# The opening of a one-layer flow-model step: transposing x one token tile at a time, with products of zeros ahead of and behind the first tile

## The chip, the cores and the metric

The kernel runs on one core of a Trainium2 chip, as one program with one launch. The metric is the device time of that core in microseconds (us), the median of several runs. TensorE (PE in the profile, with its weight loads as PEld) multiplies and transposes, VectorE (DVE), ScalarE (ACT) and GpSimd (POOL) do the elementwise work, and SyncE (SP) issues nearly all of the transfers between HBM and the on-chip memory.

## The reference

One trunk layer is applied to 128 context tokens and to 256 latent tokens, 384 in all, with a model width of 2048. Both groups have the same weights; each has its own modulation, computed from a condition vector. All of it is in 32-bit floats.

```python
mod = (silu(cond) @ ada_w + ada_b).reshape(6, 2048)      # one row set per group: cond = c_ctx, c
shift_a, scale_a, gate_a, shift_f, scale_f, gate_f = mod
h = rmsnorm(x, norm_w[0]) * (1 + scale_a) + shift_a
proj = h @ w_in                                          # q, k, v, o, gates, u
hm, C, n, m = mlstm_bidir(q, k, v, gates, C0, n0, m0)    # 8 heads x 128, both directions
hm = rmsnorm(hm, mlstm_norm_w) * sigmoid(o)
hp = pool_mixer(u, pool_w, pool_scale)                   # windows 2, 4, 8, 16
x = x + gate_a * rmsnorm(concat(hm, hp) @ w_out, norm_w[1])
h = rmsnorm(x, norm_w[2]) * (1 + scale_f) + shift_f
x = x + gate_f * rmsnorm(square(relu(h @ w1)) @ w2, norm_w[3])
```

The change touches only what stands ahead of the first products of `h @ w_in`: the transposes of x, the first parts of `silu(cond) @ ada_w`, and the order in which they come.

## The kernel before

Activations are kept transposed: 2048 channels are 16 tiles of 128 channels on the partitions, with the 384 tokens along the free axis. x arrives as three token tiles of 128 tokens by 2048 channels (`xtok`, 1 MB each: the context tokens, then two tiles of latent tokens). `transpose_x(k)` makes channel tile k: three TensorE transposes, one from each token tile, into one PSUM bank `xt`, and then one copy of 128x384 into `xT`, on VectorE for even k and on ScalarE for odd k. So every channel tile needs all three token tiles.

Each product of 32-bit floats with a weight is three products: the weight is split into a high and a low part (`hi` by ScalarE, line 135, `lo` by VectorE, line 136), and so is the activation (`hh`, `hl`).

The first stretch of the program computes `u` and `v`, two column ranges of `h @ w_in`, in eight steps s of two channel tiles each. A step has five chunks: `u` twice (512 columns), then `v` three times (3, 3 and 2 heads), 18 TensorE products each. Before a step's `h` there must be the modulation of its two channel tiles, which the generator `first_ada` computes: for channel tiles 0 and 1 eight loads of 512 KB of `ada_w` (four for the scale, then four for the shift), and for each load four products with the condition vectors on TensorE (line 257). After each four of these comes a copy `ada_sb` on ScalarE (line 269), two small products that turn the row into a column (line 273), and the additions into `mod` on VectorE (lines 281 and 286). For channel tiles 2 and 3 the same is done again with eight loads (`ada_raw_2`). The first four and the second four of these go through the same four buffers, so that each of the second four loads waits until TensorE has read the load before it out of its buffer.

`make_h` then multiplies `xT` with the scale and with 1/rms of each token (`hm`), adds the shift while splitting (`hh` on ScalarE, line 448, `hl` on VectorE, line 449), and the first `u` products follow (line 503). The 1/rms comes from the squares of x on ScalarE (line 389), is spread over the partitions by one product with a matrix of ones (`bc_rx`, line 209) and lies in `rbc`.

Until the first `u` products, the order on TensorE, VectorE and ScalarE is the order in which the code stands: the string `X_ORDER` interleaves `t` (transpose the next channel tile), `a` (the next step of `first_ada`) and `b` (`bc_rx` and its copy). Ten channel tiles are transposed there, two more inside `make_h`, and the last four after the first `u` chunk (`XT_AT = 0`). After that only TensorE's order is fixed by the code. `ADA_STEPS` says how many steps of `first_ada` follow each of the five chunks of step 0: four after the first chunk and four after the third. SyncE's queue, where all loads of x, `ada_w` and `w_in` stand one behind another, is ordered by the scheduler.

Of the kernel before, what the change touches and what calls it, by code (L numbers as in the profile page):

```python
# [30 lines left out]
XT_AT = 0  # L31
ADA_STEPS = (4, 0, 4, 0, 0)
X_ORDER = "tatatatattaatabata"
# [11 lines left out]
def hymba_kernel(  # L45
# [34 lines left out]
    nc.sync.dma_start(cc[:, 0, :], c_ctx.rearrange("(p j) -> p j", j=16))  # L80
    nc.sync.dma_start(cc[:, 1, :], c[0].rearrange("(p j) -> p j", j=16))
    nc.sync.dma_start(cst[:, 0:3], cs_src[:, 0:3])
# [4 lines left out]
    for t, src in zip(x_tok, (x_prompt[0], x_sample[0, 0:128], x_sample[0, 128:256])):  # L87
        nc.sync.dma_start(t, src)
# [16 lines left out]

    cT = adap.tile([P, 16, 38], F32, name="cT")
# [270 lines left out]
    ada0 = first_ada()  # L377
    pp = bank("pp")
    nc.tensor.transpose(pp[:, 0:96], prm[0:96, 1, :], ident[0:96, 0:96])
# [3 lines left out]

    ssq = const.tile([P, 3, 2], F32, name="ssq")
    junk = wp.tile([P, 1024], F32, tag="hi", name="junk", bufs=N_W)
    rx = const.tile([P, 3], F32, name="rx")
    for i in (0, 1, 2):
        for q in range(2):
            nc.scalar.activation(junk, x_tok[i][:, q * 1024:(q + 1) * 1024], AF.Square, accum_out=ssq[:, i, q:q + 1])

    xT_dram = dram.tile([P, KT, NTOK], F32, name="xT_dram")
    xT = []
    rbc = pre.tile([P, NTOK], F32, name="rbc")
    ss = const.tile([P, 3], F32, name="ss")
    nc.vector.tensor_reduce(ss, ssq, axis=AX.X, op=ALU.add)
    rstd_cols(rx, ss, 3, 1.0 / D)

    xt_late = []

    def transpose_x(k, later=False):  # L400
        ps = bank(f"xt_{k}")
        for i in range(3):
            nc.tensor.transpose(ps[:, i * P:(i + 1) * P], x_tok[i][:, k * P:(k + 1) * P], ident)
        t = slot(f"xT{k}")
        xT.append(t)

        def copy():
            if k % 2:
                nc.scalar.activation(t[:, 0:NTOK], ps[:, 0:NTOK], AF.Copy)
            else:  # L410
                nc.vector.tensor_copy(t[:, 0:NTOK], ps[:, 0:NTOK])

        if later:
            xt_late.append(copy)
        else:
            copy()
# [60 lines left out]
    def shift_rows():  # L477
        for _ in range(2):
            transpose_x(len(xT), True)
# [6 lines left out]
    for copy in xt_late:  # L486
        copy()
# [909 lines left out]
```

## Time and profile before

| | us |
|---|---|
| median of 3 runs (lowest, highest) | 1684.31 (1683.07, 1687.94) |
| the profiled execution's own time | 1684.17 |
| its span, first to last instruction | 1682.5 |
| TensorE busy in the span | 1654.3 (98%) |
| VectorE busy | 1340.3 (80%) |
| ScalarE busy | 751.3 (45%) |
| read from HBM | 308.61 MB |

The profile is of one execution. Each row of its time line gives the start and the length in us, the engine, the line of the kernel, the operation, the tiles written and read, and how many instructions were merged into the row; brackets hold the idle time of the engine ahead of it and what ended it. One product of plain 32-bit floats appears as two instructions of TensorE where it is not a transpose, so that the four products of one `ada` step are "x8". An instruction's length reaches to the end of its pipeline: in a run of equal ones, the distance between starts is what each costs.

### The profile page before, as it was taken

The numbers are of one execution on the slowest core, as the hardware profiler recorded it, in microseconds if no ns is written. First come the engines' busy times: TensorE is split into PE (matmuls) and PEld (weight loads), VectorE is DVE, ScalarE is ACT, GpSimd is POOL, SyncE is SP. The second block draws the span as 40 slices with busy tenths as digits, with TensorE's granted clock in tenths as the row PEclk, the third lists the DMA queues.
The fourth block names the chain that finished last, engine by engine and source line by source line (L and its number), as shares of the span: only waits on it lengthen the run. The fifth ranks groups of instructions, "written<-read, shape, count | busy, mean of one in ns | idle before, by whom it ended". The sixth has DMA issues, their size and how long they took to land.

```text
span 1682.5 us, 27870 instructions
## 1 busy us (share of the span) xinstructions
PE 1654.3 (98%) x10965; PEld 1581.4 (94%) x10965; DVE 1340.3 (80%) x2009; ACT 751.3 (45%) x1225; POOL 133.3 (8%) x185
## 2 busy tenths in 40 slices
PE   6999999999999999999999999999999999999997
PEld 3888999999999989989999999999999999999996
DVE  3677769898999959997897688988588588588688
ACT  5322355555443345543444444444444444445443
POOL 1000002221000024520000000000000000000120
PEclk9999999999999999999999999999999999999999
DMA  9999757786789954754546246444344443443653
GB/s 318 332 310 298 253 172 248 240 258 221 238 273 311 311 194 142 209 151 128 178 154 195 84 135 187 152 144 150 101 151 129 123 138 118 145 124 113 186 182 136
DMA packets 258099, 320.95 MB, mean 191 GB/s; under 512 B 14784, under 2 KB 223120, under 8 KB 257584
## 3 DMA queue, kind: packets, MB, share of 16 engines
q1 hardware_dynamic: 250688, 303.62, 57.1%
q0 software_dynamic: 5984, 13.78, 2.9%
q8 instruction: 86, 1.41, 0.4%
q10 hardware_dynamic: 1296, 1.77, 0.3%
q14 instruction: 45, 0.37, 0.1%
HBM read 308.61 MB, written 10.51 MB: 190 GB/s over the span
## 4 chain that ended last, share of the span: by engine, by line
PE 94%; DVE 3%; issue 1%; DMA 1%; ACT 0%; SPq 0%; POOL 0%; DVEq 0%; ACTq 0%; POOLq 0%
PE acc_w L145 10%; PE acc_w L144 10%; PE acc_w L146 10%; PE v L503 4%; PE y L1231 4%; PE y L1232 4%; PE y L1230 4%; PE u L503 4%; PE acc_wo L144 3%; PE acc_wo L145 3%; PE acc_wo L146 2%; PE y_yz L1231 2%; PE y_yz L1230 2%; PE y_yz L1232 2%; PE y L1074 2%; PE y L1073 2%
## 5 line engine op out<-in xcount | busy, mean ns | idle before, releaser
L145 PE MATMUL acc_w<-h2l,hi_w 128*128 128x384 f32 (+1 forms) x1024 | 346.2, 338 | 0.5 <-DVE h2l L1024 0.5
L144 PE MATMUL acc_w<-h2h,hi_w 128*128 128x384 f32 (+1 forms) x1024 | 344.2, 338 | 1.2 <-ACT h2h L1020 1.2
L146 PE MATMUL acc_w<-h2h,lo_w 128*128 128x384 f32 (+1 forms) x1024 | 345.1, 337 | 0.0
L136 DVE TENSOR_TENSOR lo_w<-raw_w,hi_w 128x1024 fp32r<-128x1024 f32 x152 | 185.3, 1220 | 136.5 <-ACT hi_w L135 136.3
L135 ACT ACTIVATE hi_w<-raw_w 128x1024 fp32r<-128x1024 f32 x152 | 160.8, 1058 | 213.7 <-PE acc_w L145 83.4
L317 DVE SCALAR_TENSOR_TENSOR ada_acc<-ada_raw,sg,ada_acc 128x1024 f32<-128x1024 f32 (+1 forms) x240 | 252.0, 1081 | 2.1 <-DMA ada_raw<-in_ada_w_dram 2.1
L144 PEld LDWEIGHTS acc_w<-h2h,hi_w 128*128 128x128 f32 x1024 | 192.2, 188 | 2.9 <-ACT h2h L1020 2.0
L145 PEld LDWEIGHTS acc_w<-h2l,hi_w 128*128 128x128 f32 x1024 | 192.6, 188 | 1.2 <-DVE h2l L1024 0.8
L146 PEld LDWEIGHTS acc_w<-h2h,lo_w 128*128 128x128 f32 x1024 | 192.4, 188 | 0.3 <-DVE lo_w L136 0.2
L1216 ACT ACTIVATE hi_t<-w 128x1024 fp32r<-128x1024 f32 x104 | 109.5, 1059 | 118.7 <-PE y L1232 34.0
L1217 DVE TENSOR_TENSOR lo_t<-w,hi_t 128x1024 fp32r<-128x1024 f32 x104 | 126.3, 1220 | 15.1 <-ACT hi_t L1216 14.7
L1217 DVE TENSOR_TENSOR lo_b<-w,hi_b 128x1024 fp32r<-128x1024 f32 x78 | 95.3, 1221 | 40.0 <-ACT hi_b L1216 39.8
L1216 ACT ACTIVATE hi_b<-w 128x1024 fp32r<-128x1024 f32 x78 | 82.5, 1060 | 97.0 <-PE acc_w L145 64.6
L135 ACT ACTIVATE hi_wo<-raw_wo 128x1024 fp32r<-128x1024 f32 x32 | 34.0, 1064 | 81.3 <-DMA raw_wo<-in_w_out_dram 64.0
L950 ACT ACTIVATE z<-acc_w 128x384 f32<-128x384 f32 x54 | 26.3, 487 | 74.8 <-PE acc_w L146 74.8
L503 PE MATMUL v<-hi_v,hh 128*128 128x384 f32 (+1 forms) x144 | 47.8, 332 | 0.0
L503 PE MATMUL v<-lo_v,hh 128*128 128x384 f32 (+1 forms) x144 | 46.5, 323 | 0.0
L503 PE MATMUL v<-hi_v,hl 128*128 128x384 f32 (+1 forms) x144 | 46.5, 323 | 0.0
L136 DVE TENSOR_TENSOR lo_wo<-raw_wo,hi_wo 128x1024 fp32r<-128x1024 f32 x32 | 38.8, 1218 | 7.3 <-ACT hi_wo L135 6.3
L986 POOL DMA_DIRECT2D gf_dram<-gfT x1 | 0.5, 521 | 551.9 <-DVE gfT L985 551.9
L144 PE MATMUL acc_k<-hh,hi_k 128*128 128x384 f32 x128 | 44.2, 345 | 0.0
L144 PE MATMUL acc_o<-hh,hi_o 128*128 128x384 f32 x128 | 43.9, 343 | 0.0
(2268 smaller groups left out, 4566.9 us busy)
## 6 DMA issues: line engine op xcount, KB each, us to landing
raw_w<-in_w_dram SPq DMA_DIRECT2D x152, 512.0 KB, 4.3
ada_raw<-in_ada_w_dram SPq DMA_DIRECT2D x130, 512.0 KB, 5.0
w<-in_w_dram SPq DMA_DIRECT2D x104, 512.0 KB, 4.4
raw_wo<-in_w_out_dram SPq DMA_DIRECT2D x32, 512.0 KB, 5.6
u<-in_ada_w_dram SPq DMA_DIRECT2D x18, 512.0 KB, 6.0
raw_u<-in_w_in_dram SPq DMA_DIRECT2D x16, 512.0 KB, 7.0
raw_q<-in_w_in_dram SPq DMA_DIRECT2D x16, 512.0 KB, 4.7
raw_k<-in_w_in_dram SPq DMA_DIRECT2D x16, 512.0 KB, 4.7
```

The lines of the kernel that those rows point to most:

```text
L135: nc.scalar.activation(hi[:, 0:n], raw[:, 0:n], AF.Copy)
L136: low = lambda: nc.vector.tensor_tensor(lo[:, 0:n], raw[:, 0:n], hi[:, 0:n].bitcast(F32), op=ALU.subtract)
L144: nc.tensor.matmul(ps, lh, rh, start=start, stop=False)
L145: nc.tensor.matmul(ps, lh, rl, start=False, stop=False)
L146: mm3.ins = nc.tensor.matmul(ps, ll, rh, start=False, stop=stop).ins
L317: nc.vector.scalar_tensor_tensor(acc[:, g, :], raw[:, a, :], cj, acc[:, g, :], op0=ALU.mult, op1=ALU.add)
L503: nc.tensor.matmul(acc[i][:, 0:n], h[k0 + k][a][:, i * P:(i + 1) * P], (hi, lo)[b][:, k, :], start=k == 0 and a + b == 0, stop=k == nk - 1 ...
L1216: nc.scalar.activation(hi, raw, AF.Copy)
L1217: nc.vector.tensor_tensor(lo, raw, hi.bitcast(F32), op=ALU.subtract)
L1230: nc.tensor.matmul(acc, xh, wh, start=start and j == 0, stop=False)
L1231: nc.tensor.matmul(acc, xh, wl, start=False, stop=False)
L1232: nc.tensor.matmul(acc, xl, wh, start=False, stop=stop and j == 3)
```

## The change

x's context tile is loaded first, ahead of the condition vectors, and the constants (the identity among them) come over ScalarE's queue instead of SyncE's. `rbc` is set to zero at the start, and six products of 128x384 zeros (`run_up(6)`) go to TensorE before x is there. `transpose_x(i, k0, on_act)` now takes one token tile i and four channel tiles: four transposes into one bank, then four copies of 128x128, and it is called for all 16 channel tiles of token tile 0, then (after two more products of zeros and the transposes of the parameters) of token tile 1, and then of tile 2. The sixteen copies of tile 0 are twelve on VectorE and four on ScalarE, those of tile 1 are all on VectorE, those of tile 2 are half and half. Only then come the steps of `first_ada`, with `bc_rx` after the third load's products. No transposes are left between or behind them. `ADA_STEPS` becomes (0, 4, 4, 0, 0): the four steps that followed the first `u` chunk now follow the second, and the other four still follow the first `v` chunk. The second `u` chunk's weights are therefore loaded ahead by one chunk only.

```diff
--- before.py
+++ after.py
@@ -28,9 +28,8 @@
 N_W = 4
 N_ADA = 4
 N_E = 1
-XT_AT = 0
-ADA_STEPS = (4, 0, 4, 0, 0)
-X_ORDER = "tatatatattaatabata"
+ADA_STEPS = (0, 4, 4, 0, 0)
+X_ORDER = "aaabaaaaaa"
 N_X = 4
 RATE_GF = 0.4
 RATE_GS = 0.25
@@ -77,15 +76,16 @@
     pre = pre_scope.enter_context(tc.tile_pool(name="pre", bufs=1))
     prm = pre.tile([P, 2, P], F32, name="prm")
     masks = vp.tile([P, N_CST - 3, P], F32, name="masks")
-    nc.sync.dma_start(cc[:, 0, :], c_ctx.rearrange("(p j) -> p j", j=16))
-    nc.sync.dma_start(cc[:, 1, :], c[0].rearrange("(p j) -> p j", j=16))
-    nc.sync.dma_start(cst[:, 0:3], cs_src[:, 0:3])
+    nc.scalar.dma_start(cst[:, 0:3], cs_src[:, 0:3])
 
     vsb = [vp.tile([P, NH, 129], F32, name=f"v{i}") for i in range(3)]
     gsb = vp.tile([P, 3, 32], F32, name="gsb")
     x_tok = [pre.tile([P, D], F32, tag=f"x{i}", name=f"xtok{i}") for i in range(3)]
-    for t, src in zip(x_tok, (x_prompt[0], x_sample[0, 0:128], x_sample[0, 128:256])):
-        nc.sync.dma_start(t, src)
+    nc.sync.dma_start(x_tok[0], x_prompt[0])
+    nc.sync.dma_start(cc[:, 0, :], c_ctx.rearrange("(p j) -> p j", j=16))
+    nc.sync.dma_start(cc[:, 1, :], c[0].rearrange("(p j) -> p j", j=16))
+    for i in (1, 2):
+        nc.sync.dma_start(x_tok[i], x_sample[0, (i - 1) * P:i * P])
     nc.gpsimd.dma_start(prm[0:96, 1, :], ada_b[0].rearrange("(r p) -> r p", p=P))
     nc.gpsimd.dma_start(prm[0:64, 0, :], norm_w[0].rearrange("i (k p) -> (i k) p", p=P))
     nc.gpsimd.dma_start(prm[64:72, 0, :], mlstm_norm_w[0].rearrange("(k p) -> k p", p=P))
@@ -103,6 +103,8 @@
     order.enter_context(tc.manual_schedule(engines={mybir.EngineType.PE, mybir.EngineType.DVE, mybir.EngineType.Activation}))
 
 
+    rbc = pre.tile([P, NTOK], F32, name="rbc")
+    nc.vector.memset(rbc, 0.0)
     cT = adap.tile([P, 16, 38], F32, name="cT")
     nc.vector.memset(cT, 0.0)
     sg = const.tile([P, 2, 16], F32, name="sg")
@@ -375,50 +377,54 @@
         yield from ada_rows([(0, k0, 2), (1, k0, 2)], ps)
 
     ada0 = first_ada()
+    ssq = const.tile([P, 3, 2], F32, name="ssq")
+    junk = wp.tile([P, 1024], F32, tag="hi", name="junk", bufs=N_W)
+    rx = const.tile([P, 3], F32, name="rx")
+    ss = const.tile([P, 3], F32, name="ss")
+    xT_dram = dram.tile([P, KT, NTOK], F32, name="xT_dram")
+    xT = [slot(f"xT{k}") for k in range(KT)]
     pp = bank("pp")
+
+    def run_up(n):
+        for _ in range(n):
+            nc.tensor.matmul(pp[:, 0:NTOK], rbc[:, 0:P], rbc, start=True, stop=True)
+
+    def squares(i):
+        for q in range(2):
+            nc.scalar.activation(junk, x_tok[i][:, q * 1024:(q + 1) * 1024], AF.Square, accum_out=ssq[:, i, q:q + 1])
+
+    def transpose_x(i, k0, on_act):
+        ps = bank(f"xt_{i}_{k0}")
+        for a in range(4):
+            nc.tensor.transpose(ps[:, a * P:(a + 1) * P], x_tok[i][:, (k0 + a) * P:(k0 + a + 1) * P], ident)
+        for a in range(4):
+            dst, src = xT[k0 + a][:, i * P:(i + 1) * P], ps[:, a * P:(a + 1) * P]
+            if on_act:
+                nc.scalar.activation(dst, src, AF.Copy)
+            else:
+                nc.vector.tensor_copy(dst, src)
+
+    run_up(6)
+    squares(0)
+    for q in range(4):
+        transpose_x(0, 4 * q, q == 3)
+    run_up(2)
     nc.tensor.transpose(pp[:, 0:96], prm[0:96, 1, :], ident[0:96, 0:96])
     nc.tensor.transpose(pp[:, 96:176], prm[0:80, 0, :], ident[0:80, 0:80])
     nc.vector.tensor_copy(prmT[:, 80:176], pp[:, 0:96])
     nc.vector.tensor_copy(prmT[:, 0:80], pp[:, 96:176])
-
-    ssq = const.tile([P, 3, 2], F32, name="ssq")
-    junk = wp.tile([P, 1024], F32, tag="hi", name="junk", bufs=N_W)
-    rx = const.tile([P, 3], F32, name="rx")
-    for i in (0, 1, 2):
-        for q in range(2):
-            nc.scalar.activation(junk, x_tok[i][:, q * 1024:(q + 1) * 1024], AF.Square, accum_out=ssq[:, i, q:q + 1])
-
-    xT_dram = dram.tile([P, KT, NTOK], F32, name="xT_dram")
-    xT = []
-    rbc = pre.tile([P, NTOK], F32, name="rbc")
-    ss = const.tile([P, 3], F32, name="ss")
-    nc.vector.tensor_reduce(ss, ssq, axis=AX.X, op=ALU.add)
-    rstd_cols(rx, ss, 3, 1.0 / D)
-
-    xt_late = []
-
-    def transpose_x(k, later=False):
-        ps = bank(f"xt_{k}")
-        for i in range(3):
-            nc.tensor.transpose(ps[:, i * P:(i + 1) * P], x_tok[i][:, k * P:(k + 1) * P], ident)
-        t = slot(f"xT{k}")
-        xT.append(t)
-
-        def copy():
-            if k % 2:
-                nc.scalar.activation(t[:, 0:NTOK], ps[:, 0:NTOK], AF.Copy)
-            else:
-                nc.vector.tensor_copy(t[:, 0:NTOK], ps[:, 0:NTOK])
-
-        if later:
-            xt_late.append(copy)
-        else:
-            copy()
+    squares(1)
+    for q in range(4):
+        transpose_x(1, 4 * q, False)
+    squares(2)
+    for q in range(4):
+        if q == 2:
+            nc.vector.tensor_reduce(ss, ssq, axis=AX.X, op=ALU.add)
+            rstd_cols(rx, ss, 3, 1.0 / D)
+        transpose_x(2, 4 * q, q >= 2)
 
     for op in X_ORDER:
-        if op == "t":
-            transpose_x(len(xT))
-        elif op == "a":
+        if op == "a":
             next(ada0)
         else:
             nc.vector.tensor_copy(rbc, bcast_row(rx, "rx")[:, 0:NTOK])
@@ -474,24 +480,15 @@
                     with tc.issue_after(load_w.ins):
                         nc.sync.dma_start(masks, cs_src[:, 3:N_CST])
 
-    def shift_rows():
-        for _ in range(2):
-            transpose_x(len(xT), True)
-        next(ada0)
-        for _ in range(2):
-            transpose_x(len(xT), True)
-
-    h_ins = make_h(0, shift_rows)
+    h_ins = make_h(0, lambda: next(ada0))
     lo_later[0]()
-    for copy in xt_late:
-        copy()
     order.close()
     order2 = ExitStack()
     order2.enter_context(tc.manual_schedule(engines={mybir.EngineType.PE}))
     for s in range(NS):
         for ci, (kind, c0, w) in enumerate(chunks):
             k0, nk = ksteps[s]
-            load_ahead(5 * s + ci, 1 if s + ci == 0 else N_AHEAD)
+            load_ahead(5 * s + ci, 1 if s == 0 and ci < 2 else N_AHEAD)
             hi, lo, n = loaded.pop(5 * s + ci)
             acc = [bank(f"{kind}_{c0}_{s}_{i}") for i in range(3)]
 
@@ -506,9 +503,6 @@
                         next(ada0, None)
             if s == ci == 0:
                 load_ahead(1, 1)
-            if s == 0 and ci == XT_AT:
-                while len(xT) < KT:
-                    transpose_x(len(xT))
             for _ in range((ADA_STEPS if s == 0 else (1, 1, 1, 0, 0))[ci]):
                 next(ada0, None)
             if ci == 3 and s < NS - 1:
```

The start of TensorE's queue, where L379 and L380 transpose the parameters, L403 (L399 after the change) x, and L257 (L259) multiplies a load of `ada_w`. Before:

```order
L379 MATMUL pp<-cst,prm 128x96
L380 MATMUL pp<-cst,prm 128x80
L403 MATMUL xt_139<-cst,xtok_89 128x128
L403 MATMUL xt_139<-cst,xtok_90 128x128
L403 MATMUL xt_139<-cst,xtok_91 128x128
L257 MATMUL ada_0_145<-ada_raw_0_0_146,cT 32x256 x4
```

and with the change:

```order
L390 MATMUL pp<-rbc 128x384 x6
L399 MATMUL xt_0_151<-cst,xtok_87 128x128 x4
L399 MATMUL xt_4_160<-cst,xtok_87 128x128 x4
L399 MATMUL xt_8_169<-cst,xtok_87 128x128 x4
L399 MATMUL xt_12_178<-cst,xtok_87 128x128 x4
L390 MATMUL pp<-rbc 128x384 x2
L412 MATMUL pp<-cst,prm 128x96
L413 MATMUL pp<-cst,prm 128x80
L399 MATMUL xt_0_195<-cst,xtok_88 128x128 x4
```

Every transpose of x now stands ahead of the first product with `ada_w`, and the first sixteen need only the context tile (`xtok_87`).

TensorE's queue between the first `u` chunk and the `v` chunks, before (a row of dots stands for further rows of the same chunk):

```order
L503 MATMUL u_0_2_312<-lo_u_0_259,hh_267 128x512
L403 MATMUL xt_337<-cst,xtok_89 128x128
...
L403 MATMUL xt_355<-cst,xtok_91 128x128
L257 MATMUL ada_2_361<-ada_raw_2_0_362,cT 32x256 x4
L257 MATMUL ada_2_361<-ada_raw_2_4_368,cT 32x256 x4
L257 MATMUL ada_2_361<-ada_raw_2_8_374,cT 32x256 x4
L257 MATMUL ada_2_361<-ada_raw_2_12_380,cT 32x256 x4
L503 MATMUL u_0_0_401<-hi_u_0_333,hh_262 128x512
...
L503 MATMUL v_0_0_432<-hi_v_0_391,hh_262 128x384
...
L257 MATMUL ada_2_361<-ada_raw_2_0_453,cT 32x256 x4
```

and with the change:

```order
L500 MATMUL u_0_2_373<-lo_u_0_344,hh_352 128x512
L500 MATMUL u_0_0_401<-hi_u_0_394,hh_347 128x512
...
L259 MATMUL ada_2_422<-ada_raw_2_0_423,cT 32x256 x4
L259 MATMUL ada_2_422<-ada_raw_2_4_429,cT 32x256 x4
L259 MATMUL ada_2_422<-ada_raw_2_8_435,cT 32x256 x4
L259 MATMUL ada_2_422<-ada_raw_2_12_441,cT 32x256 x4
L500 MATMUL v_0_0_469<-hi_v_0_452,hh_347 128x384
...
L259 MATMUL ada_2_422<-ada_raw_2_0_490,cT 32x256 x4
```

The twelve transposes are gone from there, and only one chunk (`v`, 18 products) is left between the first four and the second four `ada_2` steps, where there were two.

SyncE's queue at the loads of these second four steps (`ada_raw_2`), before:

```order
L129 DMA raw_v_0_425<-in_w_in_dram 128x2x256
L129 DMA raw_v_0_425<-in_w_in_dram 128x2x32
L253 DMA ada_raw_2_0_453<-in_ada_w_dram 128x4x256
L253 DMA ada_raw_2_4_459<-in_ada_w_dram 128x4x256
L253 DMA ada_raw_2_8_465<-in_ada_w_dram 128x4x256
L253 DMA ada_raw_2_12_471<-in_ada_w_dram 128x4x256
L129 DMA raw_u_1_482<-in_w_in_dram 128x2x512
```

and with the change:

```order
L131 DMA raw_v_0_462<-in_w_in_dram 128x2x256
L131 DMA raw_v_0_462<-in_w_in_dram 128x2x32
L368 DMA u_335<-in_ada_w_dram 128x4x256
L255 DMA ada_raw_2_0_490<-in_ada_w_dram 128x4x256
L255 DMA ada_raw_2_4_496<-in_ada_w_dram 128x4x256
L255 DMA ada_raw_2_8_502<-in_ada_w_dram 128x4x256
L255 DMA ada_raw_2_12_508<-in_ada_w_dram 128x4x256
L131 DMA raw_u_1_519<-in_w_in_dram 128x2x512
```

One load of 512 KB of a later step (`u_335`, part of the modulation of channel tiles 4 and 5, which goes to a spare place) now stands ahead of the second four; it stood seven places further behind.

## The prediction

> **What bounds the kernel now.** First the page: how busy TensorE is, and what the chain of work that ended last consists of.
>
> ```profile
> span 1682.5 us, 27870 instructions
> PE 1654.3 (98%) x10965; PEld 1581.4 (94%) x10965; DVE 1340.3 (80%) x2009; ACT 751.3 (45%) x1225; POOL 133.3 (8%) x185
> PE   6999999999999999999999999999999999999997
> PE 94%; DVE 3%; issue 1%; DMA 1%; ACT 0%; SPq 0%; POOL 0%; DVEq 0%; ACTq 0%; POOLq 0%
> ```
>
> TensorE bounds everything but the first slice (42 us) and the last. So the opening can give back at most what TensorE waits there. Next the waits of TensorE in the whole run, longest first:
>
> ```profile
> PE xt L403 <- DMA xtok<-in_x_sample_dram: 4.8, 2, 2.8
> PE pp L379 <- DMA cst<-in_consts_dram: 4.5, 1, 4.5
> PE pp L380 <- DMA prm<-in_pool_scale_dram: 4.0, 1, 4.0
> ...
> PE ada L257 <- DMA ada_raw<-in_ada_w_dram: 1.1, 1, 1.1
> ```
>
> These four, 14.4 us together, are all transfers of the opening. Third, busy time of each engine by stage, with the granted clock, the DMA share and GB/s at the end of a row:
>
> ```profile
> 0.00:16.29 16.29, 1.92 (x5) 0.84 (x5) 2.23 (x10) 7.60 (x13) 4.70 (x15) 1.00 0.85 282
> 16.29:30.00 13.71, 13.09 (x108) 6.67 (x108) 5.56 (x16) 5.11 (x11) 0.89 (x1) 1.00 1.09 356
> 37.50:45.00 7.50, 7.50 (x40) 6.48 (x36) 2.50 (x3) 4.81 (x9) 0.00 (x0) 1.00 1.03 336
> ```
>
> TensorE does 1.92 us of work in the first 16.29 us and almost never rests afterwards. But the DMA engines are full from 16 us on, at some 350 GB/s. Two queues are therefore nearly level in the opening, and work taken from TensorE counts only where the transfers are ahead of it. Fourth, TensorE's time line:
>
> ```profile
> 14.73 0.47 PE L403 MATMUL xt<-cst,xtok 128*128 128x128 f32 x1 [1.98 <-DMA xtok<-in_x_sample_dram]
> 16.32 1.08 PE L257 MATMUL ada<-ada_raw,cT 128*32 128x256 f32 x8 [1.11 <-DMA ada_raw<-in_ada_w_dram]
> 19.18 0.90 PE L403 MATMUL xt<-cst,xtok 128*128 128x128 f32 x3
> 23.15 0.64 PE L257 MATMUL ada<-ada_raw,cT 128*32 128x256 f32 x8
> 23.72 0.55 PE L403 MATMUL xt<-cst,xtok 128*128 128x128 f32 x3
> 25.38 0.91 PE L209 MATMUL bc_rx<-dg_rx,cst 128*128 128x384 f32 x2 [0.55 <-DVE dg_rx L207]
> 27.27 0.64 PE L257 MATMUL ada<-ada_raw,cT 128*32 128x256 f32 x8
> 29.84 1.83 PE L503 MATMUL u<-hi_u,hh 128*128 128x512 f32 x6
> 34.29 1.47 PE L403 MATMUL xt<-cst,xtok 128*128 128x128 f32 x12
> 35.69 1.93 PE L257 MATMUL ada<-ada_raw,cT 128*32 128x256 f32 x32
> 37.55 0.50 PE L503 MATMUL u<-hi_u,hh 128*128 128x512 f32 x1
> 41.84 0.34 PE L503 MATMUL v<-hi_v,hh 128*128 128x384 f32 x1
> 45.10 1.94 PE L257 MATMUL ada<-ada_raw,cT 128*32 128x256 f32 x32
> 46.97 0.44 PE L503 MATMUL v<-hi_v,hh 128*128 128x384 f32 x1
> ```
>
> The same eight `ada` instructions take 1.08 us at 16.32 and 0.64 at 23.15, three transposes 0.90 and 0.55: until some 20.5 us TensorE runs at 0.6 of its later rate, though the clock column says 1.00. It had worked without a rest since 16.3.
>
> **The first term: when the first u product starts.** It needs the last `ada` load, the first `raw_u` and the split of both.
>
> ```profile
> 27.84 0.88 PE L403 MATMUL xt<-cst,xtok 128*128 128x128 f32 x6
> 28.32 1.05 ACT L135 ACTIVATE hi_u<-raw_u 128x1024 fp32r<-128x1024 f32 x1
> 29.39 1.50 ACT L448 ACTIVATE hh<-hm,mod 128x128 fp32r<-128x128 f32 x4
> ```
>
> For the transfer, the answer for `raw_u` from 19.3 to 20 us:
>
> ```profile
> L129 SPq DMA_DIRECT2D raw_u<-in_w_in_dram x1: 1412/1412/1412, 19.3 to 19.3; - x1
> DMA to landing us min/median/max: 8.8/8.8/8.8
> ```
>
> Issued at 19.31 it landed at 28.1, was split from 28.32 on, ScalarE went on to `hh` at 29.39, and u started at 29.84. So u starts 1.75 us behind that landing, and the transposes that are taken away between 17 and 29 us gain nothing there: they already stood in the shadow of the transfers. What can move u is the stream itself.
>
> ```profile
> 0.81 0.38 SPq L80 DMA_DIRECT2D cc<-in_c_ctx_dram  x1
> 2.18 0.43 SPq L88 DMA_DIRECT2D xtok<-in_x_prompt_dram  x1
> 36.39 2.02 SPq L253 DMA_DIRECT2D ada_raw<-in_ada_w_dram  x4
> ```
>
> x's context tile takes the place of the first small load, 0.81 instead of 2.18, so the whole stream behind it can come up to 1.37 us earlier. The constants still have to come (192 KB, 0.5 us at 356 GB/s), on another queue but through the same engines. Bounds are 0 (other transfers set the pace of the first 10 us) and 1.37; I take 1.2, nearer to the issue rows. u starts at 28.64.
>
> **What hides the added work.** x's tiles 0 and 1 were there when their squares began:
>
> ```profile
> 7.68 1.06 ACT L389 ACTIVATE junk<-xtok 128x1024 f32<-128x1024 f32 x1 [2.94 <-DMA xtok<-in_x_prompt_dram]
> 12.32 1.06 ACT L389 ACTIVATE junk<-xtok 128x1024 f32<-128x1024 f32 x1 [2.31 <-DMA xtok<-in_x_sample_dram]
> ```
>
> Six products of zeros: `bc_rx`, the same shape, took 0.91 us, at the slow rate 0.91 x 1.08/0.64 = 1.5. From 1.5 us on (behind a memset) they end between 7 and 10.5, about when x's tile 0 is there (7.7 before, 6.5 by the shift). 32 transposes of tiles 1 and 2 cost 32 x 0.55/3 = 5.9 us, eight `ada` steps 5.1, `bc_rx` and the small products some 2: 13 us from tile 1 at some 11 us (12.3 - 1.2), done by 24; the last `ada` load, one load of 1.4 us ahead of `raw_u`, comes at 28.1 - 1.4 - 1.2 = 25.5. Without that cover (all at the slow rate) it is 13 x 1.69 = 22 us, done at 33. The copies:
>
> ```profile
> L411 DVE COPY xT<-xt 128x384 f32<-128x384 f32 x8 | 4.4, 555 | 5.0 <-PE xt L403 4.9
> L409 ACT ACTIVATE xT<-xt 128x384 f32<-128x384 f32 x8 | 3.8, 485 | 10.9 <-PE xt L403 10.9
> L381 DVE COPY prmT<-pp 128x96 f32<-128x96 f32 x1 | 0.3, 256 | 3.4 <-PE pp L380 3.4
> ```
>
> Sixteen copies of 128x384 become 48 of 128x128; between the 256 ns of 96 columns and the 555 of 384, one of 128 is about 290. VectorE gets 36, 10.4 us at most, done by some 20 us; then `dg_rx` and `bc_rx` follow by 22, and 1/rms is not needed before `hm`, at about 25. Hidden by 3 us; it would cost only what exceeds them.
>
> **The second term: behind the first u chunk.** Twelve transposes vanish: 35.69 - 34.29 = 1.40 us. With 1.2 that is a lead of 2.6 us. The chunks' costs are distances of starts: u 34.29 - 29.84 = 4.45, second u 41.84 - 37.55 = 4.29, four `ada` steps 37.55 - 35.69 = 1.86, v 45.10 - 41.84 = 3.26. Now u runs from 28.64 to 33.09, the second u to 37.38 (its VectorE split no longer stands behind two copies), the first four `ada_2` steps to 39.24, v to 42.50.
>
> **The third term: where the lead goes.** The second four `ada_2` steps come next, at 42.50 instead of 45.10. But their loads wait until TensorE has emptied the four buffers, which before began at 35.69 and now begins at 37.38, 1.69 us later. The answer for these loads from 36.3 to 38 us:
>
> ```profile
> L253 SPq DMA_DIRECT2D ada_raw<-in_ada_w_dram x4: 368/457/458, 36.4 to 37.9; - x4
> DMA to landing us min/median/max: 4.0/5.8/7.6
> ```
>
> Before: the first issued at 36.39 landed at 40.4 (4.0), the last issued at 37.95 at 45.6 (7.6), and its products were the last quarter of the row at 45.10, starting at 46.5: 0.9 us to spare. With the change: the first lands at 42.1, the last at 45.6 + 1.69 = 47.3, and TensorE, ready for it at 42.50 + 1.4 = 43.9, waits some 3.4 us in all. The last step takes 0.46, and the next v chunk starts at 47.7 instead of 46.97: 0.8 later. Against that: these four queued behind other loads before, and need 1.5 us each at the stream's rate, which is 4.0 + 3 x 1.5 = 8.5 us from the first issue (36.39 + 1.69 = 38.08) to the last landing, 46.6, where 45.6 - 36.4 = 9.2 were seen. Then the chunk starts at 47.0, as before. One further load of 512 KB now stands ahead of them; it fills the time in which SP waits, so I give it nothing (1.5 us if it is late). Between 0 and +0.8 I take +0.4. Behind this point TensorE has no wait on the opening; everything moves by that amount.
>
> **Sum.** -1.2 (stream) - 1.4 (transposes) + 3.0 (wait for the second four; between 2.6 and 3.4) = +0.4 us on the profiled execution's 1684.17, which is its span of 1682.5 and 1.7 around it, and 0.14 below the median: 1684.6. This is no change: for this kernel, about 0.3% (5 us) is what a measurement can tell, and the three runs of before lie 4.9 us apart.
>
> **The rivals.** *The lead is kept.* If the second four land in time, by an earlier stream or a shorter way than 4.0 us, all 2.6 us stay: 1681.6. For it speaks that TensorE waits for nothing later in the opening; against it the buffer rule: the first issue can't come before the first of the four steps has read its load, 38.08, and the last load cannot then be there at 43.9. Chance 0.12.
>
> *TensorE is slow again when u starts.* Its work between tile 2 and u is thin, eight steps of 0.64 in some 12 us. If it falls back to the slow rate, u's first 4.5 us (the stretch from 16.3 to about 20.8 before the rate rose) do some 2.2 us less, the second four loads go out 2.2 later still, and the time is 1686.8. Against it: between 22 and 29 us work was also broken (0.55 idle ahead of `bc_rx`) and the rate held. Chance 0.12. The Trainium skill, "TensorE: Matmul & The Clock Gate", Part 4, says that transposes do not count as activity for the clock; Part 1 says that an idle window of about 3.4 us throttles it. By it the 32 transposes would undo what the zeros bring, which makes this rival likelier; no row here separates transposes from the `ada` products beside them.
>
> *The slow rate lasts until u; the other side.* If neither zeros nor transposes raise the rate, the work of 13 us behind tile 1 takes 22, and before it eight zeros (12.3 us) and 16 transposes (4.8) end at some 18.6 instead of 11: the last `ada` step ends at 41 instead of 27.9, and u starts some 13 us late: 1697, slower than before by more than a measurement's reach. It decides once TensorE is still slow at 18 us. Against it: 4.5 us of steady work sufficed before. Chance 0.03.
>
> **How the numbers follow.** 0.73 for the forecast. The forecast and the first two rivals (0.97) lie within 5 us of before, the third rival (0.03) above. Of the 0.97 I leave 0.03 below and 0.02 above to drift between measurements, as the three runs of before show it: faster 0.03, same 0.92, slower 0.05. The range, 1681.5 to 1687.3, holds the first two rivals and the spread of before's runs.
>
> **What would show it.** Right: first u product at 28.3 to 29.8; three transposes at 0.55 us or `ada` steps at 0.64 well ahead of 20 us; no transposes behind 20 us; a new wait of TensorE for `ada_raw` of 2.5 to 3.5 us between 42 and 47.5; the third chunk's successor (the second v) at 46.5 to 47.8. Wrong: no such wait and the second v at 44.5 (first rival); `ada` steps of 1.08 behind 20 us (second and third). Anything beyond 5 us would have to come from behind the opening, where TensorE's order is the same.

## The result, and the profile after

The change made the kernel slower: a median of 1692.13 us (1691.1 to 1696.05, 6 runs) against 1684.43 (1683.07 to 1687.94, 6 runs) before, a ratio of 1.0047 with an interval of 1.0036 to 1.0059, so 6 to 10 us. The forecast was 1684.6, its range ended at 1687.3. The profiled execution took 1691.1, its span is 1689.4, 6.9 above the span before.

TensorE's waits in the whole run, after (us in total, times, longest):

```profile
PE ada L259 <- DMA ada_raw<-in_ada_w_dram: 5.9, 7, 2.4
```

The long waits for x, the constants and the parameters, 13.3 us in the first three rows of before, are down to 1.4 for x; what TensorE waits for most is now `ada_raw`, 5.9 us in seven waits (1.1 in one before). Now the stages of the opening, cut where the granted clock changes (length, busy time of TensorE, of its weight loads, of VectorE, ScalarE and GpSimd, granted clock, DMA share, GB/s):

```profile
16.75:20.17 3.42, 2.14 (x26) 0.61 (x18) 1.74 (x8) 1.50 (x10) 0.88 (x1) 1.00 1.10 349
20.17:23.58 3.41, 2.21 (x26) 0.86 (x24) 1.65 (x6) 0.38 (x1) 0.00 (x0) 1.00 1.11 350
23.58:33.82 10.24, 8.20 (x37) 4.65 (x38) 4.61 (x9) 3.77 (x7) 0.00 (x0) 0.50 1.08 357
...
37.50:45.00 7.50, 7.50 (x61) 5.75 (x60) 2.58 (x3) 4.19 (x7) 0.00 (x0) 1.00 0.52 175
...
47.47:50.89 3.42, 1.07 (x16) 0.32 (x16) 0.00 (x0) 0.00 (x0) 0.00 (x0) 1.00 1.05 375
50.89:54.30 3.41, 3.41 (x15) 3.19 (x11) 0.00 (x0) 1.44 (x2) 0.00 (x0) 0.50 1.08 363
```

The clock falls to a half twice: for 10.24 us from 23.58 on, and for 3.41 from 50.89 on. (Up to its first rise, at 6.51 here, the column reads 1.00 although the rate is the slow one.) Ahead of each fall TensorE had little to do, 2.21 of 3.41 us and 1.07 of 3.42; but the stretch from 16.75 on, with 2.14, was followed by none, so the busy time alone does not decide (last section). And between 37.5 and 45 the transfers, full before (1.03, 336 GB/s), are half idle. TensorE's time line:

```profile
21.71 0.61 PE L275 MATMUL ada<-cst,ada_sb 128*128 128x2 f32 x4 [0.50 <-ACT ada_sb L271]
22.25 0.64 PE L259 MATMUL ada<-ada_raw,cT 128*32 128x256 f32 x8
23.56 1.08 PE L259 MATMUL ada<-ada_raw,cT 128*32 128x256 f32 x8 [0.67 <-DMA ada_raw<-in_ada_w_dram]
...
28.09 1.02 PE L275 MATMUL ada<-cst,ada_sb 128*128 128x2 f32 x4 [0.56 <-ACT ada_sb L271]
29.86 2.93 PE L500 MATMUL u<-hi_u,hh 128*128 128x512 f32 x6 [0.76 <-ACT hh L454]
...
35.96 0.40 PE L500 MATMUL u<-hi_u,hh 128*128 128x512 f32 x1
...
40.25 1.93 PE L259 MATMUL ada<-ada_raw,cT 128*32 128x256 f32 x32
42.11 0.44 PE L500 MATMUL v<-hi_v,hh 128*128 128x384 f32 x1
...
45.48 1.13 PE L259 MATMUL ada<-ada_raw,cT 128*32 128x256 f32 x16
48.97 0.64 PE L259 MATMUL ada<-ada_raw,cT 128*32 128x256 f32 x8 [2.36 <-DMA ada_raw<-in_ada_w_dram]
50.46 0.72 PE L259 MATMUL ada<-ada_raw,cT 128*32 128x256 f32 x8 [0.85 <-DMA ada_raw<-in_ada_w_dram]
51.11 0.69 PE L500 MATMUL v<-hi_v,hh 128*128 128x384 f32 x1
```

Read along the places that the prediction named. u starts at 29.86 (before 29.84). Its chunk takes 6.10 us (29.86 to 35.96; before 4.45), because its first 4 us run at half clock. The first `v` starts at 42.11 (41.84), the second four `ada_2` steps at 45.48 (45.10). There TensorE waits 2.36 and 0.85, the second `v` chunk starts at 51.11 (46.97) and runs at half clock until 54.30. The first product of step 1, the first `u` row behind 50 us, before and after:

```profile
53.05 0.39 PE L503 MATMUL u<-hi_u,hh 128*128 128x512 f32 x1
```

```profile
58.62 0.39 PE L500 MATMUL u<-hi_u,hh 128*128 128x512 f32 x1
```

So the opening loses 5.57 us. The parts are u's slow start +1.65, the transposes -1.40, the wait +3.21, the way from the second `v` chunk to step 1, partly at half clock, +1.4 (7.51 in place of 6.08), and small rests, +0.7. SyncE's queue shows why the transfers pause:

```profile
34.65 0.46 SPq L368 DMA_DIRECT2D u<-in_ada_w_dram  x1
40.95 2.02 SPq L255 DMA_DIRECT2D ada_raw<-in_ada_w_dram  x4
```

From 35.1 to 40.95 it issues nothing: the first of the second four loads waits for its buffer, until TensorE has begun the first four steps (40.25, 0.70 ahead of the issue; before 35.69 and 36.39, also 0.70), and all loads behind it wait with it.

### The profile page after: what moved, and what is told of

Same layout as the page of the kernel before. It is cut to its first block, busy times and chain, and to the rows that moved or that the text cites. A ratio compares the mean times of both kernels' runs of the same rounds, so it can differ in the third digit from the quotient of the medians.

```text
span 1689.4 us, 27939 instructions
## 1 busy us (share of the span) xinstructions
PE 1665.9 (99%) x10981; PEld 1589.4 (94%) x10981; DVE 1343.8 (80%) x2038; ACT 748.8 (44%) x1229; POOL 133.3 (8%) x185
## 4 chain that ended last, share of the span: by engine, by line
PE 85%; DVE 7%; issue 3%; DMA 3%; POOL 1%; SPq 1%; ACT 1%; DVEq 0%; POOLq 0%; ACTq 0%
PE acc_w L147 10%; PE acc_w L146 10%; PE acc_w L148 10%; PE v L500 4%; PE y L1225 4%; PE y L1226 4%; PE y L1224 4%; PE u L500 4%; PE acc_wo L146 3%; PE acc_wo L147 3%; PE acc_wo L148 3%; DVE ada_acc L319 2%; PE y_yz L1225 2%; PE y_yz L1224 2%; PE y_yz L1226 2%
```

## The experiments

The theory formed on this profile: two losses, added. **Thin work**: without the transposes, TensorE has only eight short steps between 17 and 29 us, the clock falls, and u starts slow. (Before, eight channel tiles were transposed among the steps of `X_ORDER` and four in `make_h`, not ten and two as the kernel's description above has it.) **Buffers**: with one chunk instead of two between the two sets of four steps, the second four loads come late; TensorE waits, and the clock falls again. The rivals: that one of them is the whole loss, or that the eight products of zeros do harm. The edits are shown in excerpts; a row of dots stands for what is left out.

**Old places of the `ada_2` steps.**

```diff
-ADA_STEPS = (0, 4, 4, 0, 0)
+ADA_STEPS = (4, 0, 4, 0, 0)
...
-            load_ahead(5 * s + ci, 1 if s == 0 and ci < 2 else N_AHEAD)
+            load_ahead(5 * s + ci, 1 if s + ci == 0 else N_AHEAD)
```

> The changed kernel with the four ada steps back behind the first u chunk (4, 0, 4, 0, 0) and the loads ahead as before; its opening of x and zeros stays. Theory A (two causes: the clock falls before u, and the second four ada loads come too late): u starts at 29.9 and its first chunk still takes 6.1 us because the clock is low from 23.6 to 33.8, but the wait of 3 to 4 us ahead of the second v chunk is gone, and with it the second fall of the clock at 51; that chunk starts at 47 to 48 instead of 51.1, and the time is 1685.5 to 1687.5. Rival (the clock in the opening is nearly all of the loss): within 1.5 us of the changed kernel, above 1690.

Measured: 1689.06 us (1685.05 to 1690.26, 10 runs) against 1685.03, ratio 1.0016 (1.0007 to 1.0026). Two stages of the opening, and from the time line the first product of step 1:

```profile
26.56:36.79 10.23, 8.26 (x27) 5.99 (x28) 3.96 (x7) 3.76 (x7) 0.00 (x0) 0.50 1.01 327
36.80:60.00 23.20, 23.20 (x166) 18.95 (x165) 11.00 (x23) 13.96 (x27) 0.00 (x0) 1.00 0.94 307
```

```profile
55.17 0.39 PE L500 MATMUL u<-hi_u,hh 128*128 128x512 f32 x1
```

The first fall stays, 3 us later than in the change (u's chunk, from 30.62 to 37.81, loses 2.7); the wait and the second fall are gone: TensorE is busy without a gap from 36.8 to 60. Step 1 starts 2.12 later than before, in place of 5.57.

**Zeros as cover**, the steps as changed: one product of zeros (`zz`, 128x384) behind each `ada` step, the last one ahead of the first `u` product.

```diff
-X_ORDER = "aaabaaaaaa"
+X_ORDER = "azazazbazazazazazaz"
...
+        elif op == "z":
+            nc.tensor.matmul(zp[:, 0:NTOK], zz[:, 0:P], zz, start=True, stop=True)
```

> The changed kernel with one product of zeros (128x384) behind each ada step of the opening, so that TensorE has 0.64 us more to do in each 1.5 us, and one more ahead of the first u product. Theory A: the granted clock does not fall at 23.6, the ada steps stay at 0.64 us, u starts at 29.3 to 29.5 and its first chunk takes 4.45 us; the wait for the second four ada loads stays (their first load can be issued at about 39), so that the second v chunk starts at 48.5 to 49.5; time 1687.5 to 1690. Rival (the fall at 23.6 has nothing to do with how much TensorE does): the clock falls all the same, time as the changed kernel, 1691 to 1693.

Measured: 1691.59 us (1690.03 to 1692.87, 5 runs), ratio 1.0038 (1.0025 to 1.0051). The opening as one stage, and three rows of the time line:

```profile
5.60:43.00 37.40, 36.23 (x236) 22.41 (x235) 18.17 (x63) 19.64 (x43) 1.10 (x2) 1.00 0.99 320
```

```profile
45.49 0.64 PE L261 MATMUL ada<-ada_raw,cT 128*32 128x256 f32 x8 [0.77 <-DMA ada_raw<-in_ada_w_dram]
...
48.49 0.64 PE L261 MATMUL ada<-ada_raw,cT 128*32 128x256 f32 x8 [0.88 <-DMA ada_raw<-in_ada_w_dram]
...
55.15 0.39 PE L511 MATMUL u<-hi_u,hh 128*128 128x512 f32 x1
```

Now the first fall is gone and the wait stays (0.77, 0.85, 0.88). Here it comes in three shorter pieces, 2.50 us in all, and the clock does not fall behind it. Step 1 starts 2.10 late.

**Both**: the two edits together.

> Both edits: the ada steps at their old places, and products of zeros between the opening's ada steps. Theory A: no fall of the clock and no late loads: u starts at 29.4, its first chunk ends at 33.9, the second v chunk starts at 45 to 46.5, and the time is 1682 to 1684, at or a little below before. Rival (something else in the opening, such as the transposes' new place, costs the 7 us): above 1687.

Measured: 1686.51 us (1685.54 to 1690.24, 10 runs), ratio 1.0012 (1.0002 to 1.0021). The same stage and the same product:

```profile
5.10:60.00 54.90, 53.28 (x347) 36.49 (x347) 28.32 (x85) 28.64 (x61) 1.60 (x6) 1.00 1.06 342
```

```profile
52.30 0.39 PE L511 MATMUL u<-hi_u,hh 128*128 128x512 f32 x1
```

Neither loss is left; step 1 starts 0.75 earlier than before. In the profiles the losses come near to adding up: +5.57, +2.12 and +2.10 with one repair, -0.75 with both, so that either repair gains some 3.5 alone and 2.9 on top of the other. In the medians, each against the kernel before measured beside it, it is +7.7, +4.0, +6.6 and +1.5. The order of the steps bears it out (3.7 and 5.1); the cover alone (1.1) lies within the intervals, and on top of the old order it is 2.5, since the middle of the program takes part of it back (below).

The mean granted clock, which is on record for every execution, says more on the first fall. A fall of 3.41 us to a half takes 0.001 off it (3.41 x 0.5 / 1685), one of 10.24 us 0.003. The change's six executions have 0.991 to 0.994, the five with cover 0.995 to 0.999, the ten with both 0.997 or 0.998. With the old places alone nine of ten have 0.993 or 0.994 and took 1687.51 to 1690.26 us; the tenth has 0.997, and took 1685.05, as before does.

**No products of zeros**, all else as changed: `run_up(6)` and `run_up(2)` taken out.

> The changed kernel without the eight products of zeros; nothing else. If transposes count as activity for the clock as products do, it rises during the 32 transposes of x's tiles 1 and 2, by 17 us at the latest, and sixteen transposes take 1.9 us there at some point. If they do not count (as the Trainium skill has it, TensorE: Matmul & The Clock Gate, Part 4), it is still at half at 17 us and rises only when the u products run, at 31 to 35 us; the ada steps then take 1.08 us throughout.

Measured: one execution, 1689.31 us. Two rows of its time line (the constants come at 6.94), then two stages:

```profile
6.94 3.68 PE L399 MATMUL xt<-cst,xtok 128*128 128x128 f32 x16 [6.94 <-DMA cst<-in_consts_dram]
...
57.58 0.39 PE L498 MATMUL u<-hi_u,hh 128*128 128x512 f32 x1
```

```profile
12.67:19.50 6.83, 4.96 (x51) 3.21 (x49) 5.79 (x30) 5.36 (x16) 0.88 (x1) 1.00 1.09 356
19.50:33.15 13.65, 11.64 (x58) 6.64 (x59) 5.93 (x15) 4.15 (x8) 0.00 (x0) 0.50 1.09 356
```

The clock rises at 12.67 behind nothing but transposes, of x and of the parameters, and falls at 19.50. Step 1 starts 4.53 late, near the change's 5.57: in this one execution the zeros neither cause nor cure the loss. The Trainium skill, "TensorE: Matmul & The Clock Gate", Part 4, says that transposes do not count as activity for the clock; here, and in 32 bits, they raise it.

**Real work as cover**: the old steps, and six groups of four transposes of tiles 0 and 2 between the `ada` steps. Behind tile 0's first group stand four products of zeros in place of two behind the whole tile, and VectorE makes all copies.

```diff
+X_ORDER = "axaaxbaxaaxaxaxa"
...
+    x_left = [(0, 4), (2, 4), (0, 8), (2, 8), (0, 12), (2, 12)]
...
+        elif op == "x":
+            transpose_x(*x_left.pop(0))
```

> The old order of the ada_2 steps, and real work as cover: six groups of four transposes (tile 0's and tile 2's later channels) stand between the ada steps of the opening; no product of zeros behind tile 1. Theory of cover (the clock falls when TensorE works less than about 0.45 of one window of 3.41 us, whatever the work is): clock 1.0 from about 6 us to 62, u starts at 29.3 to 29.8 and its chunk takes 4.45, no wait over 0.5 at the second four ada_2 loads; offset against before -1.2 to -1.9 at 58 us, and 1682.5 to 1684.5 us if that offset lasts to the end, up to 1686.5 if the middle loses 2.5 as it did with zeros as cover. Rival (transposes do not hold the clock): it falls between 20 and 27 us, the u chunk takes 6 us or more, offset about +2, 1687 to 1689 us.

Measured: 1687.26 us (1686.2 to 1690.61, 11 runs) against 1686.08, ratio 1.0011 (1.0002 to 1.002). The profiled execution is the slowest of these; its stages, and the row of `bc_rx`:

```profile
13.37:16.78 3.41, 2.01 (x20) 1.15 (x24) 3.06 (x18) 2.80 (x6) 0.07 (x1) 1.00 1.09 359
16.78:20.20 3.42, 1.74 (x20) 0.61 (x16) 1.40 (x8) 0.00 (x0) 0.82 (x1) 1.00 1.10 349
```

```profile
20.83 1.65 PE L211 MATMUL bc_rx<-dg_rx,cst 128*128 128x384 f32 x2 [1.44 <-DVE dg_rx L209]
```

The edit brought a wait of its own: VectorE came to `dg_rx` late, behind the copies of the transposes, `bc_rx` held TensorE up for 1.44 us, and the clock fell behind that window (1.74 of 3.42 us busy), at 20.20. Step 1 starts 4.02 late. So the profile doesn't decide between the theory and its rival. The other ten executions have a granted clock of 0.995 to 0.997, where without cover nine of ten had 0.993 or 0.994: it seems that transposes as cover hold the clock longer in most executions, but no profile shows one.

**The second four steps one chunk later** (`ADA_STEPS = (0, 4, 0, 4, 0)`), the rest as changed.

> The change as it is, but with the second four ada_2 steps one chunk later (0, 4, 0, 4, 0 in place of 0, 4, 4, 0, 0). If the second half of the loss is the wait for these four loads, whose buffers come free too late, and the fall of the clock behind that wait: the first fall stays (u chunk about 6 us), the waits at the second four go to under 0.5 in all, the clock does not fall near 51 us, offset at 58 us +1.5 to +2.5 in place of +5.5, 1686.5 to 1689 us. Rival (the loads are late for another reason, or the clock falls there anyway): offset +4 or more, 1690 to 1692 us.

Measured: 1694.85 us (1693.05 to 1695.35, 4 runs), ratio 1.0053 (1.004 to 1.0067): against the theory's number, and no better than the change (8.8 above before, the change 7.7). SyncE's queue, a stage, and the row of the wait:

```profile
34.87 0.46 SPq L368 DMA_DIRECT2D u<-in_ada_w_dram  x1
43.12 0.37 SPq L131 DMA_DIRECT2D raw_u<-in_w_in_dram  x1
43.59 2.34 SPq L255 DMA_DIRECT2D ada_raw<-in_ada_w_dram  x4
```

```profile
37.50:45.00 7.50, 7.50 (x59) 5.53 (x59) 2.59 (x3) 4.62 (x8) 0.00 (x0) 1.00 0.28 67
```

```profile
50.23 0.64 PE L259 MATMUL ada<-ada_raw,cT 128*32 128x256 f32 x8 [1.98 <-DMA ada_raw<-in_ada_w_dram]
```

A later consumer does not cure the wait, because the order of the loads changed with it. Behind the load into `u` SyncE stands still for 7.8 us at a `raw_u`, which now comes ahead of the second four, and issues these at 43.59, 2.6 later than in the change. What costs is that the one queue stops at a load that can't start yet, while the transfers lie idle (0.28). Step 1 starts 7.30 late.

**Zeros on the kernel before**: six products ahead of its first transpose, nothing else.

> The kernel before with one thing added: six products of zeros on TensorE ahead of its first transpose. Theory (the transfers set the pace of the opening, TensorE's rate there is worth nothing as long as it is not slow at u): clock up 10 us or more earlier than 20.8, the transposes and ada steps of 16 to 20 us short, but u at 29.8 as before, no fall behind it (TensorE is still about 0.8 busy), 1683.5 to 1685.5 us, the same. Rival (an earlier clock brings time): u 0.5 or more earlier, 1682 to 1683.5 us. Other rival (it falls back in the opening): u chunk over 5.5 us, 1686 us or more.

Measured: 1687.97 us (1686.28 to 1689.95, 10 runs), ratio 1.0012 (1.0003 to 1.0021); not the 1683.5 to 1685.5 expected. Two stages and the product:

```profile
9.50:12.91 3.41, 0.33 (x1) 0.14 (x1) 0.07 (x1) 1.07 (x3) 0.00 (x0) 1.00 0.90 364
12.91:19.74 6.83, 4.11 (x23) 1.62 (x23) 0.79 (x3) 4.36 (x9) 0.88 (x1) 0.50 1.07 357
```

```profile
52.65 0.39 PE L507 MATMUL u<-hi_u,hh 128*128 128x512 f32 x1
```

The early clock is lost again by 12.91, in the wait for tile 1, and is back at 19.74, a little before the 20.8 of before. Step 1 starts 0.40 earlier. So the loss, 1.9 us in the median and 4.3 in the profile from step 1 to the end, came behind the opening, where the order of the instructions is that of before: in the profile, 1.4 near 370 and 390 us, 1.6 at 542 with a fall of the clock, and 1.4 near 880.

**Lighter cover**: both edits, with zeros of 128 columns in place of 384.

> The kernel with the old order of the ada_2 steps and zeros as cover, but with products of 128 columns in place of 384: about a third of the added work, some 0.15 us per step, so that TensorE works about 0.5 of each window of the thin stretch in place of 0.7. If the limit lies between 0.44 and 0.49, as the runs so far have it: clock 1.0 through the opening, u at 29.5 to 29.9 (no long product ahead of it), its chunk 4.45, offset -1.0 to -1.7 at 58 us, 1682.5 to 1686 us. Rival (the limit is higher, or the kind of work counts): the clock falls between 20 and 27 us, u chunk 6 us or more, offset about +2, 1687 to 1689.5 us.

Measured: 1687.92 us (1685.89 to 1688.91, 11 runs) against 1686.08, ratio 1.0011 (1.0002 to 1.002). A stage of the opening and two of the middle, then a row of the time line:

```profile
17.73:31.38 13.65, 11.60 (x86) 6.43 (x86) 5.88 (x17) 4.77 (x11) 0.88 (x1) 1.00 1.09 356
...
536.56:539.97 3.41, 2.66 (x22) 2.58 (x21) 3.41 (x8) 1.95 (x5) 0.00 (x0) 1.00 1.08 375
539.97:543.38 3.41, 3.41 (x12) 3.41 (x12) 3.41 (x7) 1.43 (x5) 0.00 (x0) 0.50 1.06 366
```

```profile
50.81 0.39 PE L511 MATMUL u<-hi_u,hh 128*128 128x512 f32 x1
```

The opening is the best of all: the clock stays up, step 1 starts 2.24 us early. And yet the time is not better than before. In this profile 1.9 of the lead are left at 530 us; 1.6 go at 540, where the clock falls for 3.41 us behind a stretch of 4-column products (`ada_gate`, `adaf`); and 2.7 more go between 800 and 905, in part where TensorE waits for VectorE's splits (1.50 at 889.97; before, at the same product, 0.63). VectorE is busy without a gap there, from 872 to 892, but so it is before: why the waits are longer is not shown.

**The stretch near 540 us filled**: two products of 384 columns, whose result nobody reads, ahead of `ada_gate`'s small ones; on lighter cover, and on the kernel before.

> The kernel with light cover, and two products of 384 columns whose result nobody reads, ahead of the small products of ada_gate near 537 us, so that the thin stretch there (2.6 us of 4-column products and a wait of 0.75) is filled. Theory (a window of 3.41 us that holds this stretch whole makes the clock fall for one window, 1.7 us each): no fall of the clock near 540 us, the granted clock of most executions 0.001 higher than with light cover alone, offset against before -1.5 to -2.2 still at 600 us, time 0.5 to 1.7 below light cover alone: 1684.5 to 1687 us where before takes 1685 to 1686. Rival (the middle loses the lead whatever the clock does, to VectorE's queue or to transfers): offset at 900 us +1.5 or more, time within 0.5 of light cover alone, 1687.5 to 1688.5 us.

> The kernel before with those two products alone. Theory: its executions with a granted clock of 0.997 (17 of 47 so far, against 0.998 for nearly all others) become rare, the spread narrows, time 0 to 0.8 below before. Rival (the fall near 540 us has another cause, or the two products cost more than they save): as many executions at 0.997, or time 0.3 to 1 above before.

Measured: 1689.31 us (1686.19 to 1691.69, 12 runs) and 1688.45 (1685.19 to 1689.72, 11 runs) against 1685.81, ratios 1.0014 (1.0006 to 1.0022) and 1.001 (1.0002 to 1.0019). Both take longer than before, and the first no less than lighter cover without the filling (3.5 above before, against 1.8). In the second the clock still fell near 540 us:

```profile
544.70:548.11 3.41, 3.41 (x13) 3.41 (x12) 3.41 (x4) 1.13 (x5) 0.00 (x0) 0.50 1.09 350
```

The products moved the stretch by 1.3 us instead of filling it: its inner gap (0.75, waiting for ScalarE) stayed. The first kept its clock there and lost time elsewhere, beginning in the opening, where the clock fell from 31.10 to 34.51. So light cover does not hold the clock in every execution, and filling that stretch brought nothing. The times lie even above those that the rivals gave (1687.5 to 1688.5, and 0.3 to 1 above before; measured 2.6 above).

**Lighter cover without the eight zeros at the start.**

> The kernel with light cover, without the eight products of zeros at the start. Theory (those eight only bring the clock's rise forward, into time in which TensorE waits for transfers): clock up at 10 to 18 us in place of 5 to 8, by the transposes and what follows them, and held by the cover; u starts at 28.8 to 30 as with them, its chunk 4.45, offset at 58 us -0.5 to -2.3, time within 1 us of light cover, 1685.5 to 1688.5 us. Rival (without the zeros the clock is not up, or falls, when u starts): u chunk 5.5 us or more, offset 0 or more, 1688.5 us or more.

Measured: 1686.22 us (1683.99 to 1688.65, 10 runs) against 1685.81, ratio 1.0 (0.9991 to 1.0009): the only variant that is level with before. Three stages:

```profile
24.53:27.94 3.41, 2.02 (x20) 0.85 (x20) 0.00 (x0) 0.26 (x1) 0.00 (x0) 1.00 1.05 372
27.94:31.36 3.42, 2.44 (x13) 1.76 (x13) 1.60 (x5) 3.11 (x7) 0.00 (x0) 1.00 1.09 349
31.36:34.77 3.41, 3.41 (x10) 2.63 (x9) 2.36 (x3) 0.52 (x1) 0.00 (x0) 0.50 1.01 324
```

So the zeros at the start bring nothing. The profiled execution contradicts a part of the theory, a limit on the busy time of a window: its clock held behind a window with 2.02 us of work and fell behind the next, with 2.44. None of the variants is faster than the kernel before.

## Why the prediction was wrong

**The first term (the stream, -1.2) came out at nothing.** Only the context tile came up by 1.37 us in the queue; the loads behind it moved up by less, the first `ada_w` load by 0.06. So 1.37 was the bound for one load, not for the stream. Its row before and after, then the answer for `raw_u` from 18 to 40 us, after:

```profile
3.61 15.66 SPq L253 DMA_DIRECT2D ada_raw<-in_ada_w_dram  x8
```

```profile
3.55 15.55 SPq L255 DMA_DIRECT2D ada_raw<-in_ada_w_dram  x8
```

```profile
L131 SPq DMA_DIRECT2D raw_u<-in_w_in_dram x2: 710/1062/1414, 19.1 to 20.6; - x2
DMA to landing us min/median/max: 8.5/8.6/8.6
```

Issued at 19.15, the first landed at 27.75, 0.34 earlier, not 1.2: of the two bounds, 0 and 1.37, the lower one was the nearer. And u stood 2.1 behind the landing, not 1.75: the last `ada` rows, on which it also hangs, ran at half clock (1.08 and 1.02 us; with lighter cover, at the full clock, u stands some 1.75 behind again). In the nine variants of the changed opening that landing lies between 27.1 and 28.5.

**"What hides the added work" failed, and with it the likeliest case.** The step took all added and moved work as hidden, and found it done by 24; it did not ask what is left for TensorE between the loads once the transposes are gone. The rival "TensorE is slow again when u starts" had the place, the sign (`ada` steps of 1.08 behind 20 us) and nearly the price (2.2; u's chunk cost 1.65), at a chance of 0.12. What I set against it, that work before was also broken from 22 to 29 us, misread the row: from 16.29 to 30.00 it had 13.09 us of work in 13.71, after the change 9.18. The transposes that "gain nothing there" when taken away gave TensorE the work that kept the clock up. With products of zeros of 384 columns in their place this is shown; with transposes themselves it is only indicated (real work as cover). The last rival did not come: the clock was up at 6.51.

**The third term had the right size, but the path around it was wrong.** The wait was sized at 2.6 to 3.4 and measured 3.21. But u's late end moved it: the second four were issued at 40.95, not 38.08. The second `v` was to start at 47.7 at the latest and started at 51.11, because the lead that was to pay for the wait (2.6) was not there. And the idle time brought the second fall (+1.4), which no term had. That the load of a later step ahead of them "fills the time in which SP waits" was too kind: SyncE stood still for 5.8 us, and the transfers idled, which the step did not see as a cost of a buffer in one ordered queue.

**The second term held**: in the sum of the result it stands as it was, 1.40 for twelve transposes.

**"Everything moves by that amount" held for 300 us.** Step 1 starts 5.57 late, and at 360 us TensorE is 5.6 late; at the end 6.8. In between come +1.1 near 370 and 390 us, +1.6 at 549 (a fall of the clock), -0.9 between 870 and 905, and small amounts that come to -0.6. For a lead it fails: lighter cover's 2.24 had turned into 2.4 late by 900 us. The rivals were priced one at a time; slow clock and late loads came together, and the range did not allow for that.

## What to carry to other kernels

Before taking work off an engine whose clock depends on how busy it is, read what is left there per 3.4 us: transposes that seem mere filler may hold the rate for what follows. When two steps that share buffers move closer together, follow the one queue that loads them: its first blocked load stops all behind it. A lead won in the opening is worth measuring where it is won (the start of a later step) and again at the end, since a stretch bound by another engine can take it back.

## What the runs showed of the hardware

**The clock moves on a grid of 3.41 us.** After: up at 6.51, down 23.58, up 33.82, down 50.89, up 54.30; the distances are 5, 3, 5 and 1 times 3.413. Its phase differs from execution to execution: with the same six products at the start the first rise lies between 5.07 and 7.49 us over nine profiles. The Trainium skill, "TensorE: Matmul & The Clock Gate", Part 1, calls the window free-running, which agrees; it has an idle window throttle the clock, and here windows with 1.07, 2.21 and even 2.66 us of work in 3.41 did so. Sorted by busy time, the windows of the thirteen openings at the full clock show a pattern. All eight with 1.80 us or less were followed by a fall, none with 2.5 or more. In between, from 1.87 to 2.44, four were and eleven were not, and what parts these is the kind of work: each of the four holds a group of 2- or 4-column products (0.61 us, as the row at 21.71 above), none of the eleven does. The window with 2.66, near 540 us, also consists in good part of 4-column products. So small products seem to count for little; no run varied them alone.

**The same place loses a window in some executions and not in others.** The `ada_gate` stretch near 540 us brought a fall, which costs 1.6 us, in nine of thirteen profiles; the profile of before is one of the four without. The 76 executions of before beside the experiments have a granted clock of 0.998 in 50 (median 1685.13) and 0.997 in 23 (1687.01), 1.9 us apart, which is about one such fall. That each of these is that fall is argued, not shown: the profile of lighter cover has the fall and 0.998, since the clock's last fall, at the end of the program, also differs in length.

**Openings vary by themselves.** Step 1 starts at 53.05 in the profile of before and at 54.03 in that of the kernel with the filled stretch, whose opening is the same; and at 50.81 and 53.57 with lighter cover, without and with the filling. So an offset from one profile is good to about 1 to 3 us; the 2.9 to 3.5 of each repair stand above it only just, and rest on the rows (the fall, the wait, and their absence), on the granted clocks and on the medians as well. Why the zeros on the kernel before, and the leads, lose 2 to 4 us in the middle is open: waits for VectorE's splits between 800 and 905 us and the fall at 540 are places seen, and no run changed the first alone.
